# w_in of the first attention in two stages: 13 outputs summed over all k tiles as the modulation arrives, then the query blocks

## The chip, the cores and the metric

The kernel runs on one core of one Trainium2 chip. The metric is the device time of one execution in microseconds (us). All weights and activations are float32 in HBM; TensorE (PE) multiplies, VectorE (DVE) and ScalarE (ACT) work on SBUF and PSUM, SyncE (SP) issues the DMA transfers from one queue.

## The reference

Three layers run on 256 tokens of 2048 features. The first is the one that the change touches:

```python
mod = silu(c) @ w_mod + b_mod                     # c: one row of 2048; mod: 6 x 2048
sh1, sc1, g1, sh2, sc2, g2 = split(mod, 6)
h = rms_norm(x, norm_attn) * (1.0 + sc1) + sh1    # 256 x 2048
qa, ka, va, qb, ckv, qi, ki, wi = split(h @ w_in) # 2048 x 3664
out_a = swa_attention(qa, ka, va, sinks, rel_a)   # 16 heads of 64, window 128
out_b = dsa_attention(qb, rms_norm(ckv, kv_norm), w_uk, w_uv, qi, ki, wi, rel_b)
x = x + g1 * (concat(out_a, out_b) @ w_out)
h = rms_norm(x, norm_ffn) * (1.0 + sc2) + sh2
x = x + g2 * conv_ffn(h, w_up, conv_w, conv_b, w_down)
```

dsa_attention scores all keys with 16 index heads (qi, ki, wi), keeps the 64 best keys of each query, and attends to these with 16 heads. After this come a gMLP layer and an MLA layer with modulations of their own (from a second row c_2).

## The kernel before

Activations lie transposed: 16 tiles of 128 features by 256 tokens. To reach float32 accuracy at the speed of the rounded type, each operand is split in a high and a low part. Weights come in loads of 1 MB (`load`, five buffers with the tag raw, shared by all weights); `parts` splits 1024 columns with one ScalarE copy (L327) and one VectorE subtraction (L328); five buffers each hold high and low parts, two and a half blocks of weights. `product` then runs three matmuls per k tile of 128 and output block of 128 (L338 to L340). A full block of 128 outputs over 16 k tiles is 48 matmuls of 256 columns.

The modulation vectors are 14 vectors of 2048 (MODS), each 16 MB of weights. `mod_part` computes 128 entries of one: it loads 1 MB in the buffers with the tag raw and VectorE multiplies and sums it (L448). Eight of the 16 column groups of sc1, which the first product needs, are computed otherwise: `mod_first` multiplies the column c by w_first on PE, with one output row (L462, 32 matmuls of 512 columns, each in two passes as plain float32), and turns the row to columns with small matmuls (L472). `mod_rest` is the list of all other modulation parts, in the order of MODS; `step(rate)` takes so many parts of the list as the rate says at each weight block, `need(name)` takes all that is left of one vector. The parts issue their loads in the same SP queue as the weights.

`setup` computes sc1's and sh1's first eight column groups and the root of the mean square of x (squares on ScalarE, added on VectorE, L313; summed over partitions by PE, L303; then `rsqrt`, `diagonal`, `row`). `first_attention` runs w_in in two halves over k: 14 pairs of output blocks (`half_blocks`, w[0, i]) and the 80 outputs of ki and wi over k tiles 0 to 7, kept in SBUF (part); then, when the other halves of sc1 and sh1 are there, the same over k tiles 8 to 15 (`final`), and VectorE adds the first half (L738). In the second half the index scores (`index`), the selection (`top`), the attention generators (`attend`: scores and softmax, transposes, values with two heads in two halves of PE's columns, L644 and L646), and the keys and values of the second attention (`keys_of`, `values`) are worked in between the pairs. Two pairs of the second half run as plain float32 without a split (WIN). Then w_out runs in two halves with the second attention's eight head pairs in between, and the FFN opens with `shifts` and `opening`, whose first products have 258 columns and need all of sh2.

The program's framework orders the instructions of each engine at build time by a priority list and its own costs; each engine then works through its order, and a semaphore holds it where an operand or a buffer is missing.

Of the kernel before, what the change touches and what calls it, by code (L numbers as in the profile page):

```python
# [21 lines left out]
P = 128  # L22
# [16 lines left out]
WIN, WOB = (6, 8), (0, 2)  # L39
# [3 lines left out]
RP0, RP1, RWA, RWB, RF, RG, RM = 1.0, 1.7, 2.0, 1.0, 0.82, 0.5, 0.6  # L43
# [3 lines left out]

MODS = ["sc1", "sh1", "g1", "sc2", "sh2", "g2", "shA", "scA", "gA", "kvsh", "kvsc", "shB", "scB", "gB"]
# [11 lines left out]
def _layout(a):  # L60
# [19 lines left out]
    m["w_first"] = c(ws["sc1"][:, :1024].reshape(8, 2, P, 1024).transpose(0, 2, 1, 3)).reshape(8, P, 2048)  # L80
# [18 lines left out]
    for w in range(3):  # L99
# [18 lines left out]
    m["w_kiwi"] = c(kiwi.reshape(2, 8, P, 80).transpose(0, 2, 1, 3)).reshape(2, P, 8 * 80)  # L118
    m["w_in"] = c(np.concatenate([qi, ckv, ka, va, qa, qb], 1).reshape(2, 8, P, 14, 2, P).transpose(0, 3, 2, 4, 1, 5)
                  ).reshape(2, 14, P, 2048)  # L120
# [78 lines left out]
class Build:  # L199
# [253 lines left out]
    def mod_first(self):  # L453

        nc = self.nc
        banks = [self.bank(), self.bank()]
        for q in range(8):
            raw = self.load(self.ap["w_first"][q])
            for e in range(2):
                k = 2 * q + e  # L460
                for j in range(2):
                    nc.tensor.matmul(banks[j][:1], self.cact[:, k:k + 1],  # L462
                                     raw[:, e * 1024 + j * 512:e * 1024 + j * 512 + 512],
                                     start=k == 0, stop=k == 15)
            if q < 7:
                yield
        line = self.tmp("s", (1, 1024))
        for j in range(2):
            nc.scalar.copy(line[:, j * 512:j * 512 + 512], banks[j][:1])
        ps = self.bank()  # L470
        for b in range(8):
            nc.tensor.matmul(ps[:, b:b + 1], line[:, b * P:(b + 1) * P], self.ones[:1, :1], start=True, stop=True)  # L472
        nc.vector.tensor_add(self.mod_tile("sc1")[:, :8], ps[:, :8], self.vec("b_sc1", 0, 8))
        self.mod["sc1"][1] += 8
        yield

    def mod_rest(self):
        for j in range(8, DB):
            for name in ("sc1", "sh1"):
                self.mod_part(name, j)  # L480
                yield
        for name in MODS[2:]:
            for j in range(DB):
                self.mod_part(name, j)
                yield
# [167 lines left out]
    def setup(self):  # L653
# [4 lines left out]
        self.cact = self.con.tile([P, DB], F32, name="cact")  # L658
        nc.scalar.activation(self.cact, self.vec("c", 0, DB), AF.Silu)
        self.c_src = None  # L660
        a = self.mod_first()
        self.X = self.con.tile([P, DB, T], F32, name="X")
        self.acc = self.con.tile([P, T], F32, name="ssacc")
        for q in range(8):
            next(a)
            self.mod_part("sh1", q)
            if q == 1:
                nc.sync.dma_start(self.X, self.ap["xT"])
                self.ident = self.load_const("ident")
            if q == 3:  # L670
                for k in range(DB):
                    self.add_square(self.acc, self.X[:, k], k == 0)
                self.R = self.row(self.diagonal(self.rsqrt(self.token_sums(self.acc), 2, 1.0 / D)))
# [20 lines left out]
    def first_attention(self):  # L694
        nc, ap = self.nc, self.ap
        with self.tc.tile_pool(name="pa", bufs=1, reuse_waits="tile") as pool:
            g1a = self.gain(self.vec("norm_attn", 0, 8), self.mod_tile("sc1")[:, :8], "gg1a")
            xs = self.modulated(self.R, g1a, self.mod_tile("sh1"), range(8))
            w, wk = ap["w_in"], ap["w_kiwi"]
            isc = 64 ** -0.5 * 16 ** -0.5  # L700

            def kiwi(half, xs):
                raw = self.load(wk[half], 640)
                ps = self.bank()
                self.product(ps[:80], self.parts(raw, 0, 640), xs, width=80)
                self.step(0.6)
                return ps

            scale = lambda i: 0.125 if i >= 6 else 1.0
            ps = kiwi(0, xs)  # L710
            keys = self.pair()
            kw = keys[:80, 0]
            nc.scalar.activation(kw[:64], ps[:64, :T], AF.Copy)
            nc.scalar.activation(kw[64:], ps[64:80, :T], AF.Copy, scale=isc)
            part = []
            for i in range(14):
                pp = self.half_blocks(w[0, i], xs, RP0)
                part.append(self.pair())
                for e in range(2):
                    self.evac(part[i][:, e], pp[e], scale(i), which=1)  # L720
                if i == 3:
                    self.tables(pool)
            self.need("sc1"), self.need("sh1")
            g1b = self.con.tile([P, DB], F32, name="gg1b")
            nc.vector.scalar_tensor_tensor(g1b[:, 8:], self.mod_tile("sc1")[:, 8:], 1.0,
                                           self.vec("norm_attn", 8, 8), op0=OP.add, op1=OP.mult)
            xf = []
            xs = self.modulated(self.R, g1b, self.mod_tile("sh1"), range(8, 16), xf)
            rate = RP1
# [109 lines left out]
            for j in range(8):  # L839
# [17 lines left out]
                if j == 5:  # L857
                    keys_of(0)
# [474 lines left out]
```

## Time and profile before

| what | value |
|---|---|
| median of three runs | 2306.7 us (2305.6 to 2308.2) |
| profiled execution, its own time | 2308.6 us |
| its span, first to last instruction | 2306.9 us |
| busy PE, DVE, ACT | 97%, 81%, 50% of the span |
| mean granted clock of TensorE | 0.988 of full |
| DMA | 629.6 MB, 273 GB/s over the span |

The span leaves out 1.7 us of the execution's own time. Busy time counts pipelined matmuls from their start to a modelled end; a busy PE can still work at a lower granted clock, which is listed beside it. Lines with an L are lines of the kernel before. A matmul of plain float32 shows as two passes. In the rows of windows the busy times stand in the order PE, weight loads of PE (PEld), DVE, ACT, POOL, each with its count of instructions.

### The profile page before, as it was taken

Reading aid. Unit: us, or ns where it says so; the run is one execution under the profiler, and the core shown is the slowest. Engines: PE = TensorE matmul, PEld = TensorE weight load, DVE = VectorE, ACT = ScalarE, POOL = GpSimd, SP = SyncE. Lnnn points to the kernel's source line nnn. Section 1 sums busy time; section 2 is a strip of 40 time slices with the busy share of each in tenths; the row PEclk is TensorE's granted clock in tenths of the full one; section 3 lists DMA queues with packets and bytes.
Section 4 is the critical chain, followed back from the end, with each engine's and each line's share of the span. In section 5 each row is a group of like instructions: output and inputs, shape, how many; then the busy total and the mean of one; then the engine's idle time right before and its main releaser. Section 6 shows DMA issues by size and latency. Waiting matters only on the chain.

```text
span 2306.9 us, 42375 instructions
## 1 busy us (share of the span) xinstructions
PE 2248.1 (97%) x17326; PEld 2130.1 (92%) x17326; DVE 1869.0 (81%) x3043; ACT 1151.2 (50%) x1917; POOL 4.0 (0%) x8
## 2 busy tenths in 40 slices
PE   7988999999999999999999999999999999999999
PEld 1987888999999999999998889999999999899899
DVE  4889998999898888888898769777776568766784
ACT  2543675665444444444675444435344457455552
POOL 0000000000000000000000000000000000000000
PEclk8999999999999999999999999999999999999999
DMA  9898798889998999898677776887775555344342
GB/s 372 341 355 330 281 378 315 307 331 338 340 358 316 333 360 344 300 360 342 210 251 285 280 276 249 288 285 272 279 274 191 185 187 179 136 156 156 138 147 92
DMA packets 97764, 629.57 MB, mean 273 GB/s; under 512 B 10945, under 2 KB 18081, under 8 KB 28961
## 3 DMA queue, kind: packets, MB, share of 16 engines
q1 hardware_dynamic: 97570, 626.87, 73.7%
q8 instruction: 135, 2.21, 0.4%
q14 instruction: 59, 0.48, 0.1%
HBM read 624.68 MB, written 2.15 MB: 272 GB/s over the span
## 4 chain that ended last, share of the span: by engine, by line
PE 88%; DVE 8%; ACT 2%; issue 1%; DMA 1%; SPq 0%; DVEq 0%; ACTq 0%
PE bank L339 24%; PE bank L338 24%; PE bank L340 24%; PE bank L405 4%; PE bank L404 4%; PE bank L406 4%; DVE mraw L448 2%; DVE wl L328 2%; PE bank L462 1%; DMA raw<-in_w_first_dram 1%; PE bank L1019 1%; PE bank L594 1%; ACT wh L327 1%; PE bank L386 0%; DVE ssacc L313 0%
## 5 line engine op out<-in xcount | busy, mean ns | idle before, releaser
L338 PE MATMUL bank<-act,wh 128*128 128x256 f32 (+2 forms) x4976 | 1411.5, 284 | 15.3 <-ACT wh L327 9.3
L339 PE MATMUL bank<-act,wh 128*128 128x256 f32 (+1 forms) x4976 | 1405.4, 283 | 0.6 <-DVE act L259 0.3
L340 PE MATMUL bank<-act,wl 128*128 128x256 f32 (+2 forms) x4976 | 1399.0, 282 | 4.3 <-DVE wl L328 4.3
L327 ACT ACTIVATE wh<-raw 128x1024 fp32r<-128x1024 f32 (+2 forms) x760 | 759.9, 1007 | 672.7 <-PE bank L339 493.7
L328 DVE TENSOR_TENSOR wl<-raw,wh 128x1024 fp32r<-128x1024 f32 (+2 forms) x760 | 874.8, 1160 | 213.7 <-ACT wh L327 211.3
L338 PEld LDWEIGHTS bank<-act,wh 128*128 128x128 f32 (+1 forms) x4976 | 942.6, 190 | 24.7 <-ACT wh L327 10.8
L340 PEld LDWEIGHTS bank<-act,wl 128*128 128x128 f32 (+1 forms) x4976 | 941.4, 189 | 6.2 <-DVE wl L328 6.1
L339 PEld LDWEIGHTS bank<-act,wh 128*128 128x128 f32 (+1 forms) x4976 | 943.7, 190 | 1.9 <-DVE act L259 1.6
L448 DVE CUSTOM_DVE_ANT_0 mraw<-mraw,c_all,k_vecs 128x2048 f32<-128x2048 f32 x216 | 506.4, 2346 | 47.0 <-DMA mraw<-in_wmods_dram 25.9
L404 PE MATMUL bank<-wh,act 128*128 128x512 f32 (+1 forms) x392 | 152.0, 388 | 0.0
L405 PE MATMUL bank<-wl,act 128*128 128x512 f32 (+1 forms) x392 | 151.6, 387 | 0.0
L406 PE MATMUL bank<-wh,act 128*128 128x512 f32 (+1 forms) x392 | 151.1, 385 | 0.0
L258 ACT ACTIVATE act<-t 128x256 fp32r<-128x256 f32 x158 | 63.6, 414 | 95.5 <-DVE t L916 52.3
L404 PEld LDWEIGHTS bank<-wh,act 128*128 128x128 f32 x392 | 73.7, 188 | 15.5 <-PE bank L1223 1.0
L406 PEld LDWEIGHTS bank<-wh,act 128*128 128x128 f32 x392 | 73.7, 188 | 15.0 <-issue 0.7
L405 PEld LDWEIGHTS bank<-wl,act 128*128 128x128 f32 x392 | 73.8, 188 | 14.9 <-issue 0.7
L259 DVE TENSOR_TENSOR act<-t,act 128x256 fp32r<-128x256 f32 x158 | 64.7, 424 | 15.7 <-ACT act L258 15.1
L905 ACT ACTIVATE t<-bank,k_vecs 128x256 f32<-128x256 f32 x41 | 23.0, 560 | 70.6 <-PE bank L340 70.6
L567 DVE SCALAR_TENSOR_TENSOR X<-bank,m_g,X 128x256 f32<-128x256 f32 x96 | 46.1, 481 | 7.4 <-PE bank L340 5.3
L567 DVE SCALAR_TENSOR_TENSOR X<-bank,m_gA,X 128x256 f32<-128x256 f32 x64 | 30.8, 481 | 18.4 <-PE bank L340 18.4
L462 PE MATMUL bank<-raw,cact 128*1 128x512 f32 x64 | 36.1, 723 | 9.3 <-DMA raw<-in_w_first_dram 9.3
L909 ACT ACTIVATE t<-t 128x256 f32<-128x256 f32 x44 | 18.3, 416 | 52.4 <-DVE t L907 52.4
(230 smaller groups left out, 1214.4 us busy)
## 6 DMA issues: line engine op xcount, KB each, us to landing
mraw<-in_wmods_dram SPq DMA_DIRECT2D x216, 1024.0 KB, 6.6
raw<-in_w_up_dram SPq DMA_DIRECT2D x88, 1024.0 KB, 6.6
raw<-in_w_down_dram SPq DMA_DIRECT2D x64, 704.0 KB, 5.7
raw<-in_w_u_dram SPq DMA_DIRECT2D x32, 1024.0 KB, 5.2
raw<-in_w_v_dram SPq DMA_DIRECT2D x32, 1024.0 KB, 4.9
raw<-in_w_z_dram SPq DMA_DIRECT2D x32, 1024.0 KB, 5.0
raw<-in_w_ao_dram SPq DMA_DIRECT2D x32, 1024.0 KB, 4.9
raw<-in_w_in_dram SPq DMA_DIRECT2D x28, 1024.0 KB, 7.2
```

What stands on the lines that cost most here:

```text
L258: self.nc.scalar.activation(hi, src, AF.Copy)
L259: self.nc.vector.tensor_sub(lo, src, hi.bitcast(F32))
L327: nc.scalar.activation(h[:, :n], raw[:, lo:hi], AF.Copy)
L328: nc.vector.tensor_sub(l[:, :n], raw[:, lo:hi], h[:, :n].bitcast(F32))
L338: mm(ps[:, :n], h[:, s], x[:, :n], start=first and k == 0, stop=False)
L339: mm(ps[:, :T], h[:, s], x[:, LO:], start=False, stop=False)
L340: mm(ps[:, :n], l[:, s], x[:, :n], start=False, stop=last and k == len(xs) - 1)
L404: mm(ps, xh, h[:, s], start=k == 0, stop=False)
L405: mm(ps, xh, l[:, s], start=False, stop=False)
L406: mm(ps, xl, h[:, s], start=False, stop=k == kt - 1)
L448: self.nc.vector.tensor_tensor_reduce(out=raw, in0=raw, in1=self.c_all, scale=1.0, scalar=self.vec("b_" + name, j), op0=OP.mult, op1=OP.ad ...
L567: self.nc.vector.scalar_tensor_tensor(self.X[:, b], ps[:, :T], gate[:, b:b + 1], self.X[:, b], op0=OP.mult, op1=OP.add)
```

## The change

w_in is laid out anew. Its first 13 output blocks (index queries, compressed keys, k and v of the first attention, ki and wi) are w_a, one load of 1616 columns per k tile. Seven PSUM banks hold their sums over all 16 k tiles: `tile_of(k)` runs 39 matmuls for k tile k as soon as its operand is there, and sc1's and sh1's parts for k are loaded in between. Then 16 query blocks (w_q), each over all 16 k tiles, run one by one with index scores, selection and the first attention in between; keys and values of the second attention come after them. Half of sc1 and all of g1 are computed on PE by `mod_cols`: a load holds four k tiles by 512 columns, its four matmuls have 32 output rows each (one of them not zero) and write four 32-partition strips of one bank; small matmuls against a column of ones sum the strips and turn them to columns. The squares of x are summed by PE over k. The lists of steps follow: one part per query block, g1 first. In the cut diff, `modulated` scales k tiles and makes their operands, and `taken` copies a pair of sums out of PSUM.

```diff
-WIN, WOB = (6, 8), (0, 2)
+WOB = (0, 2)
-RP0, RP1, RWA, RWB, RF, RG, RM = 1.0, 1.7, 2.0, 1.0, 0.82, 0.5, 0.6
+RP, RWA, RWB, RF, RG, RM = 1.0, 2.0, 1.0, 0.82, 0.5, 0.6
+WA = 1024 + 256 + 128 + 128 + 80
+COLS = ["sc1", "g1"]
...
-    def mod_first(self):
+    def mod_cols(self, name, q):
...
+        bank = self.bank()
+        for i in range(4):
+            raw = self.load(self.ap["w_cols"][COLS.index(name), q, i])
+            for e in range(4):
+                nc.tensor.matmul(bank[32 * e:32 * e + 32], self.cact[:, 4 * i + e], raw[:, e * 512:e * 512 + 512],
+                                 start=i == 0, stop=i == 3)
+            if i < 3:
                 yield
-        line = self.tmp("s", (1, 1024))
-        for j in range(2):
-            nc.scalar.copy(line[:, j * 512:j * 512 + 512], banks[j][:1])
+        line = self.pair().rearrange("p a b -> p (a b)")
+        nc.scalar.copy(line, bank)
...
+        for b in range(4):
+            nc.tensor.matmul(ps[:, b:b + 1], line[:, b * P:(b + 1) * P], self.ones[:, :1], start=True, stop=True)
+        s = slice(4 * q, 4 * q + 4)
+        nc.vector.tensor_add(self.mod_tile(name)[:, s], ps[:, :4], self.vec("b_" + name, 4 * q, 4))
+        self.mod[name][1] += 4
...
     def mod_rest(self):
+            if name in COLS:
+                for q in range(4):
+                    yield from self.mod_cols(name, q)
...
-        a = self.mod_first()
...
-        for q in range(8):
+        a = self.mod_cols("sc1", 0)
+        for q in range(4):
             next(a)
             self.mod_part("sh1", q)
...
+            if q == 1:
+                ss = self.bank()
                 for k in range(DB):
-                    self.add_square(self.acc, self.X[:, k], k == 0)
-                self.R = self.row(self.diagonal(self.rsqrt(self.token_sums(self.acc), 2, 1.0 / D)))
+                    sq = self.tmp()
+                    nc.scalar.activation(sq, self.X[:, k], AF.Square)
+                    for tb in range(2):
+                        nc.tensor.matmul(ss[:, tb:tb + 1], sq[:, tb * P:(tb + 1) * P], self.ones[:, :1],
+                                         start=k == 0 and tb == 0, stop=k == DB - 1 and tb == 1)
+                self.R = self.row(self.diagonal(self.rsqrt(ss[:, :2], 2, 1.0 / D)))
...
-        self.cact = self.con.tile([P, DB], F32, name="cact")
+        self.cact = self.con.tile([P, DB, 32], F32, name="cact")
+        nc.vector.memset(self.cact, 0.0)
+        nc.scalar.activation(self.cact[:, :, 0], self.vec("c", 0, DB), AF.Silu)
...
+            sums = [self.bank() for _ in range(7)]
+
+            def tile_of(k):
+
+                raw = self.load(ap["w_a"][k], WA)
+                x = xs[k]
+                hl = [self.parts(raw, 0, 1024), self.parts(raw, 1024, WA)]
+                for i in (12, *range(12)):
+                    h, l = hl[i // 8]
+                    n = 80 if i == 12 else P
+                    s = slice(i % 8 * P, i % 8 * P + n)
+                    ps = sums[i // 2][:n, i % 2 * T:i % 2 * T + T]
+                    mm = nc.tensor.matmul
+                    mm(ps, h[:, s], x[:, :T], start=k == 0 and i % 2 == 0, stop=False)
+                    mm(ps, h[:, s], x[:, LO:], start=False, stop=False)
+                    mm(ps, l[:, s], x[:, :T], start=False, stop=k == DB - 1 and (i % 2 == 1 or i == 12))
+
+            modulated(range(4))
+            a = self.mod_cols("sc1", 1)
+            for k in range(4):
+                tile_of(k)
+                next(a)
+                self.mod_part("sh1", 4 + k)
+            modulated(range(4, 8))
+            self.tables(pool)
+            done = 4
+            for k in range(8, DB):
+                self.mod_part("sc1", k)
+                self.mod_part("sh1", k)
+                modulated(range(k, k + 1))
+                for _ in range(2):
+                    if done < k:
+                        tile_of(done)
+                        done += 1
+            tile_of(DB - 1)
+
...
-            part = []
-            for i in range(14):
...
-            def final(i, turned=False, between=None):
...
+            qis = [taken(i, True) for i in range(4)]
+            kv = taken(5, False)
+            ckv = taken(4, False)
...
+            def query(n, between=None):
+
+                if n % 2 == 0:
+                    q_pairs.append(self.pair())
+                ps = self.bank()
+                hl = self.weights(ap["w_q"][n], DB, rate)
+                self.product(ps, hl[0], xs[:8], True, False)
+                if between is not None:
+                    between()
+                self.product(ps, hl[1], xs[8:], False, True)
+                nc.scalar.activation(_turned(q_pairs[n // 2][:, n % 2]), _two(ps[:, :T]), AF.Copy, scale=0.125)
...
-            gens = [first(0), first(1)]
-            for j in range(8):
...
+            gens = []
+            for n in range(16):
+                p = n - 5
+                query(n, (lambda: next(gens[p])) if 0 <= p < 8 else None)
+                if 0 <= p < 8:
+                    mix.append(next(gens[p]))
+                if n < 4:
+                    index(n, qis[n])
+                elif n < 8:
+                    top(2 * n - 8)
+                    top(2 * n - 7)
...
+                if 3 <= n < 11:
+                    gens.append(first(n - 3))
+            keys_of(0)
+            gens.append(second(0))
+            values()
+            gens.append(second(1))
+            keys_of(1)
```

## Rows read from the trace of the kernel before

**Rows 1.** Windows: stretch, length, busy us of five engines, granted clock, DMA share, GB/s.

```profile
0.00:59.00 59.00, 43.83 (x94) 10.14 (x94) 29.54 (x53) 12.79 (x29) 0.20 (x4) 0.88 0.92 373
59.00:152.00 93.00, 87.29 (x698) 85.18 (x698) 78.41 (x87) 47.29 (x82) 0.00 (x0) 0.96 0.91 349
152.00:309.00 157.00, 137.43 (x1004) 121.35 (x1006) 152.04 (x331) 87.27 (x216) 0.00 (x0) 0.92 0.86 319
309.00:378.00 69.00, 67.91 (x562) 59.15 (x558) 64.09 (x138) 48.85 (x139) 0.00 (x0) 1.00 0.94 352
378.00:429.00 51.00, 48.54 (x357) 46.47 (x353) 47.73 (x73) 28.21 (x54) 0.00 (x0) 1.00 0.82 309
480.00:900.00 420.00, 420.00 (x3558) 420.00 (x3557) 374.97 (x448) 199.09 (x267) 0.00 (x0) 1.00 0.91 340
```

**Rows 2.** Timeline: start, length, engine, line, operation, count, [wait before and its releaser].

```profile
30.63 1.02 PE L303 MATMUL bank<-ones,ssacc 128*128 128x1 f32 x4 [3.71 <-DVE ssacc L313]
...
38.11 0.37 ACT L297 COPY row<-bank 128x256 f32<-128x256 f32 x1 [11.85 <-PE bank L295]
...
56.87 0.17 DVE L473 TENSOR_TENSOR m_sc<-bank,k_vecs 128x8 f32<-128x8 f32 x1 [0.42 <-PE bank L472]
...
59.39 0.34 PE L338 MATMUL bank<-act,wh 128*80 128x256 f32 x1 [2.56 <-ACT act L258]
...
155.80 0.50 PE L338 MATMUL bank<-act,wh 128*80 128x256 f32 x1 [7.47 <-ACT wh L327]
...
309.40 0.38 PE L338 MATMUL bank<-act,wh 128*128 128x256 f32 x1
...
428.91 0.39 PE L338 MATMUL bank<-act,wh 128*128 128x258 f32 x1 [1.85 <-ACT act L538]
```

**Rows 3.** The page's costliest groups, VectorE.

```profile
L328 DVE TENSOR_TENSOR wl<-raw,wh 128x1024 fp32r<-128x1024 f32 (+2 forms) x760 | 874.8, 1160 | 213.7 <-ACT wh L327 211.3
...
L448 DVE CUSTOM_DVE_ANT_0 mraw<-mraw,c_all,k_vecs 128x2048 f32<-128x2048 f32 x216 | 506.4, 2346 | 47.0 <-DMA mraw<-in_wmods_dram 25.9
...
L259 DVE TENSOR_TENSOR act<-t,act 128x256 fp32r<-128x256 f32 x158 | 64.7, 424 | 15.7 <-ACT act L258 15.1
```

**Rows 4.** Windows of 20 us: clock and DMA in busy stretches.

```profile
40.00:60.00 20.00, 14.58 (x46) 4.16 (x45) 10.57 (x15) 3.84 (x8) 0.00 (x0) 1.00 1.00 410
100.00:120.00 20.00, 18.82 (x159) 18.61 (x158) 15.37 (x14) 9.96 (x15) 0.00 (x0) 1.00 1.01 419
140.00:160.00 20.00, 11.30 (x84) 10.72 (x83) 17.86 (x25) 14.22 (x27) 0.00 (x0) 0.81 0.91 333
220.00:240.00 20.00, 14.45 (x90) 12.50 (x90) 19.97 (x73) 11.11 (x34) 0.00 (x0) 0.74 0.90 350
```

**Rows 5.** Timeline, PE: one load of w_first.

```profile
45.98 3.59 PE L462 MATMUL bank<-raw,cact 128*1 128x512 f32 x8 [0.95 <-DMA raw<-in_w_first_dram]
```

**Rows 6.** Timeline, PE: products in two column groups and the next form.

```profile
238.41 0.65 PE L644 MATMUL bank<-pT,va 128*64 128x256 f32 x4
238.89 0.39 PE L646 MATMUL bank<-pT,va 128*64 128x128 f32 x4
239.21 0.49 PE L585 MATMUL bank<-pair 64*128 64x128 f32 x4
```

**Rows 7.** Groups of instructions by line, VectorE, 152 to 309 us.

```profile
L448 DVE CUSTOM_DVE_ANT_0 mraw<-mraw,c_all,k_vecs 128x2048 f32<-128x2048 f32 x27 | 63.1, 2343 | 0.0
...
L738 DVE SCALAR_TENSOR_TENSOR pair<-bank,pair 128x256 f32<-128x256 f32 x28 | 11.6, 420 | 1.7 <-PE bank L340 1.4
```

**Rows 8.** Groups of instructions by line, VectorE, 309 to 428 us.

```profile
L448 DVE CUSTOM_DVE_ANT_0 mraw<-mraw,c_all,k_vecs 128x2048 f32<-128x2048 f32 x21 | 49.2, 2343 | 0.0
```

**Rows 9.** Timeline, SP: the first load of w_up.

```profile
412.53 0.33 SPq L319 DMA_DIRECT2D raw<-in_w_up_dram  x1
```

## What the change will do to the time

> **What bounds the kernel now.** I read the view by windows first, cut at the stage borders, because shares over the whole span hide that only the first fifth is not bound by TensorE. From 480 us on PE is busy all the time: 3558 matmuls in 420 us, 0.118 us each, so a full block of 48 costs 5.67 us [rows 1]. Nothing in the change touches that part, except one load more or less of lead. What the change can win lies ahead of 429 us, and the timeline gives the borders [rows 2]: the first product of w_in starts at 59.4, the second half of w_in at 155.8 (after 7.5 us of waiting), w_out at 309.4, the opening of the FFN at 428.9. Three things bind there. Up to 59 us it is transfers: 373 GB/s, and PE is busy with single-row sums. From 152 to 309 it is VectorE: 152.0 busy of 157, while PE stands still for 20 us and much of its busy time runs at a granted clock of 0.92 of full [rows 1]. From 309 to 429 PE binds again, 116.5 of 120 us, but VectorE is close behind it with 111.8 [rows 1]. So a gain ahead of 309 reaches the end, provided that VectorE does not get more to do behind 309.
>
> **The change part by part.** All times are on the span's clock; the profiled execution took 2308.6 us (span 2306.9), the median of the runs is 1.9 us lower.
>
> *Setup.* The modulation that the first product needs shrinks from eight loads of w_first and eight of sh1 to four and four. With X and the vectors that is 10.8 MB, 29 us at 373 GB/s [rows 1], where the old sums ended at 57.0 [rows 2]. The sum of squares leaves VectorE (15 additions) for 64 one-column passes on PE. Four such passes took 1.02 us at a low clock [rows 2], so they cost at most 16 us, beside loads. X lands earlier, as its load now stands ahead of the second block of w_cols; I let the squares begin at 16 and the sum end near 32. From there the old chain to the row of roots took 6.8 us (31.65 to 38.48) [rows 2]. With 2.5 us to the first operand (56.87 to 59.39 before) the first tile starts at 41 instead of 59.4. The roots, not the modulation, are then late.
>
> *First stage, w_in's 13 outputs.* PE needs 16 x 39 x 0.118 = 74 us, VectorE per late k tile two modulation sums of 2.35, splits of 1.2 and 0.7 and twice 0.42 for the operand [rows 3], 7.4 us. Loads: up to the fourth tile 22.5 MB in all, at 373 GB/s 60 us; then 16 blocks of modulation and 12 of w_a, 26.7 MB. Their rate lies between the 419 and the 333 GB/s of busy windows [rows 4]: 64 to 80 us; I take 370, 72 us, so that the last block lands at 132. Per k tile that is 7.9 us of transfer against 7.4 of VectorE and 4.6 of PE: the loads set the pace. Behind them stand one sum (2.35), the last operand (2.5), the last tile (4.6) and 1.5 us for a clock that falls in the gaps: the stage ends at 143 (135 to 152).
>
> *Second stage, queries.* The old window has 137.4 us of PE busy at a clock of 0.92, some 126 at full clock. Its 14 half products and the small one were 82, so index scores, attention, keys and values are 44 [rows 1]. The new stage has 16 blocks (90.7), the same 44, and gate g1: 16 loads of four matmuls, each to another 32 columns of the array. Nothing before writes four column groups, so I bound it. The upper end is the old form, one row: 3.59 us per load of eight passes [rows 5]. The lower end comes from attention's products, which write two column groups: four passes of 256 columns take 0.48 us until the next product starts, where the one-row form (0.449 per pass of 512) would take 0.90 [rows 5, 6]. So groups do run side by side; four groups make 0.96 per load. The shorter products behind them take 0.32 instead of half of 0.48 until a product of another form starts, 0.08 for the switch [rows 6]; two switches make 1.12 per load, 18 us. The Trainium skill speaks against the change here: TensorEngine Tiling (Array Packing), Key Properties, says that a change of tiling mode drains TensorE. The row agrees, at 0.08 us a time. With 3 us for the little products that turn g1 into columns, PE has 156 us. VectorE loses 27 modulation sums (63.1) and 28 additions (11.6) [rows 7] and gains eight splits (10): 87 of 157 us, no longer the bound. ScalarE's cost (copies out of PSUM instead of two evacuations) lies beside PE: it is busy 87 of 157 [rows 1]. I add 4 us of waits, as the old kernel has between 309 and 429 [rows 1], and take off 2 because query 0 needs only operands 0 to 7 for its first half and can fill the wait for the last one. w_out starts at 143 + 158 = 301 instead of 309.4.
>
> *The background list.* This is the price. Sixteen query steps use up exactly g1's sixteen loads. The sixteen of sc2 come in w_out's first half, eight of sh2 in its second, and the last eight are forced by need("sh2") right ahead of the FFN, in front of w_up on SP's queue. The old kernel ran 21 modulation sums behind 309 (49.2 us) [rows 8]; the new one must run 32, less what SP's five raw buffers let it do early. The weights of queries, keys and w_out that fill these buffers leave a sum little to wait for, so I take 8 done early. Then VectorE has 111.8 - 49.2 + 24 x 2.35 = 119.0 us beside PE's 119.5: two engines that are both full don't fit without loss; I take 5 us (0 to 18; 18 is with nothing early, 62.6 + 75.2 = 137.8). The queue says the same: w_up's first load left 16.4 us before its product started [rows 2, 9], and eight loads of 1.05 MB take 22.5 us at 373 GB/s.
>
> *Sum.* 301 + 119.5 + 5 = 425.5 against 428.9: 3.4 us earlier, the rest of 1878 us unchanged. 2308.6 - 3.4 = 2305.2 for an execution like the profiled one, 2303 for a median.
>
> **The rivals.**
> 1. *The forced loads bite* (slower). VectorE has done nothing early, so 13 us more stand ahead of the FFN: 2316. For it: VectorE is 94% busy from 378 on [rows 1] and SP issues in order. Against it: PE sets the pace of the second stage, so sums that need only VectorE should run ahead there. It decides against the change below about six sums done early: (32 - 6) x 2.35 + 62.6 is 4 us over PE's time, and with the 5 us of friction that eats the 8.4 won before.
> 2. *The column groups don't overlap*, so that gate g1 costs PE what mod_first did: 16 x (3.59 - 1.12) = 40 us more, 2343. The two-group rows speak against it [rows 6].
> 3. *Loads run at the upper rate* and VectorE has slack. At 410 to 419 GB/s [rows 4] the blocks land 13 us earlier, VectorE then holds the stage to 7 of these, and the FFN opens without the 5 us: 2290. For it: such rates stand where only large rows move. Against it: five buffers, shared by weights that wait for PE.
> 4. *The clock falls in the first stage.* Where PE was busy 14.5 of 20 us the granted clock was 0.74, and 0.81 around the wait of 7.5 us [rows 4]; at 0.74 a tile takes 6.2 us, still under the 7.9 between tiles, and only the last one counts. At the low level, 1.2 GHz, a tile takes 9.2 us, and five late tiles and the last one lose 5 x 1.3 + 4.6 = 11 us: 2313. The Trainium skill, TensorE: Matmul & The Clock Gate, HAM oscillation, tells of a loop over k tiles with a transfer to wait for that runs every tile cold; the old kernel's rows fall only in part.
>
> **How the numbers follow.** 0.2% of this kernel, 4.6 us, is about what a measurement tells from no change. The forecast, 2303, has 0.50; its own terms (end of the first stage 135 to 152, opening 0 to 9) spread it over 0.24 faster, 0.22 same, 0.04 slower. Rival 1 has 0.18, rival 2 0.07, rival 3 0.17, rival 4 0.08 (0.02 of it same). That makes faster 0.41, same 0.24, slower 0.35. The range leaves out rival 2 and the tail beyond rivals 1 and 3: 2286 to 2324; the forecast's own range is 2292 to 2313, since its two terms seldom stand at the same end.
>
> **What would show it.** In the new profile: the first product of a tile near 41; the last tile's end near 143 with a DMA share over 0.9 until then; four one-row matmuls of a load within about 1.1 us (rival 2: 3.6); VectorE under 65% busy in the queries, PE over 95%; residuals of w_out starting near 304; the wait ahead of the 258-column products under 7 us (rival 1: 15 or more). I am wrong if the planner's order holds TensorE on a load or a bank that this arithmetic does not see, above all in the first stage, where seven of eight banks are taken.

## The result: 40 us slower

The changed kernel takes 2346.3 us (median of 4 runs, 2345.8 to 2347.9) against 2306.7 (2305.6 to 2308.2): a ratio of 1.0173, interval 1.0155 to 1.0190. The forecast was 2303, range 2286 to 2324. It failed, and the sign with it: a gain was forecast, and the kernel is 1.7% slower.

The windows of the changed kernel, cut at its own stage borders (setup, first stage, queries, w_out, and the stretch behind 480 that [rows 1] also has):

```profile
0.00:49.00 49.00, 30.89 (x115) 19.02 (x116) 15.33 (x35) 14.57 (x33) 0.20 (x4) 0.97 0.75 292
49.00:166.00 117.00, 93.08 (x674) 84.86 (x677) 88.55 (x111) 42.00 (x69) 0.00 (x0) 0.87 0.91 349
166.00:330.00 164.00, 158.82 (x1272) 132.66 (x1265) 99.14 (x267) 98.17 (x242) 0.00 (x0) 0.98 0.73 264
330.00:466.00 136.00, 114.89 (x904) 104.65 (x902) 128.04 (x216) 73.84 (x182) 0.00 (x0) 0.94 0.90 333
480.00:900.00 420.00, 419.41 (x3547) 418.93 (x3546) 376.30 (x468) 208.29 (x289) 1.67 (x2) 1.00 0.90 335
```

Behind 480 nothing has changed. The queries are TensorE's, as forecast (158.8 busy of 164). The first stage is nobody's: PE 93, VectorE 89 of 117 us, 349 GB/s. From w_out on VectorE leads, 128.0 of 136.

The borders in the changed kernel's timeline answer [rows 2]. The second line is the first residual of w_out, which began 3.2 us after w_out's first product before (312.6 and 309.4), so that w_out starts near 329.6 (an estimate from these rows):

```profile
48.78 0.50 PE L728 MATMUL bank<-act,wh 128*80 128x256 f32 x1 [4.72 <-ACT wh L331]
332.76 0.45 DVE L568 SCALAR_TENSOR_TENSOR X<-bank,m_g,X 128x256 f32<-128x256 f32 x1
466.02 0.58 PE L342 MATMUL bank<-act,wh 128*128 128x258 f32 x1 [20.99 <-ACT act L539]
```

First tile 48.8 (forecast 41), w_out 329.6 (301; 309.4 before), opening of the FFN 466.0 (425.5; 428.9 before). The opening is 37.1 us late, the spans differ by 37.2: all of the loss lies ahead of 466. (The medians differ by 39.7: the profiled execution of before stood 1.9 above its median, that of the change 0.6 below.) Of the 37.1, 20.2 stand at w_out's start and 16.9 come between there and the opening.

**Three places where it goes.** First, setup. VectorE's timeline:

```profile
18.53 0.22 DVE L683 CAST identb<-k_ident 128x128 bf16<-128x128 f32 x1
32.38 0.16 DVE L271 TENSOR_SCALAR rs_x<-bank 128x2 f32<-128x2 f32 x1 [13.63 <-PE bank L678]
...
34.23 2.35 DVE L452 CUSTOM_DVE_ANT_0 mraw<-mraw,c_all,k_vecs 128x2048 f32<-128x2048 f32 x1
...
47.31 0.08 DVE L452 DVE_READ_ACCUMULATOR2_ANT m_sh<- 128x1 f32 x1
```

The first operation of the root waits 13.6 us for the squares' sums on TensorE, at its place in VectorE's fixed order, and sh1's second sum stands behind it. Its raw buffer stays held, and the loads stop: SP issues only three from 8.6 to 36.6. The row of roots came when forecast (38.8), but sh1's fourth sum was done only at 47.3.

Second, the late k tiles: VectorE, ScalarE and SP's queue in one period of 8.60 us (from one k tile's multiply-add on ScalarE, L519, to the next one's):

```profile
115.15 0.33 SPq L323 DMA_DIRECT2D raw<-in_w_a_dram  x1
...
123.83 2.35 DVE L452 CUSTOM_DVE_ANT_0 mraw<-mraw,c_all,k_vecs 128x2048 f32<-128x2048 f32 x1
...
126.22 0.60 ACT L519 ACTIVATE t<-t,m_sh,gg 128x256 f32<-128x256 f32 x1 [6.15 <-DVE m_sh L452]
126.73 1.04 ACT L331 ACTIVATE wh<-raw 128x1024 fp32r<-128x1024 f32 x1
...
127.80 1.23 DVE L332 TENSOR_TENSOR wl<-raw,wh 128x1024 fp32r<-128x1024 f32 x1 [1.27 <-ACT wh L331]
```

The w_a tile issued at 115.15 lands some 6.2 us later, at 121.4 (the next one, issued at 123.75, can't be the one split at 126.7). ScalarE is idle, but at the head of its order stands the multiply-add of the next operand, which waits for VectorE's sum until 126.2. Then VectorE waits 1.27 us for wh; that is nearly all the idle time it has in the period, and with its own 7.3 us of work it makes the 8.60. The tile holds one of five raw buffers meanwhile.

Third, the opening. SP's queue, whose w_up load left at 412.5 before [rows 9]:

```profile
421.48 0.33 SPq L323 DMA_DIRECT2D raw<-in_w_out_dram  x1
425.31 28.19 SPq L449 DMA_DIRECT2D mraw<-in_wmods_dram  x9
455.44 11.87 SPq L323 DMA_DIRECT2D raw<-in_w_up_dram  x6
```

Nine modulation loads in a row, paced by VectorE's sums through the raw buffers, and w_up behind them: TensorE stands 21.0 us. What ends the wait is the last sum of sh2 and not w_up: ScalarE has split the first w_up load from 460.8 on, and then waits for VectorE to make the operand of the 258-column products from sh2:

```profile
464.54 0.22 ACT L536 ACTIVATE shift<-m_sh 128x16 fp32r<-128x16 f32 x1 [2.69 <-DVE m_sh L452]
```

### The profile page after: what moved, and what is told of

Its sections match the earlier page's. It is cut to its first block, busy times and chain, and to the rows that moved or that the text cites. A ratio compares the mean times of both kernels' runs of the same rounds, so it can differ in the third digit from the quotient of the medians.

```text
span 2344.1 us, 42822 instructions
## 1 busy us (share of the span) xinstructions
PE 2261.0 (96%) x17578; PEld 2148.6 (92%) x17578; DVE 1826.3 (78%) x2989; ACT 1155.0 (49%) x1926; POOL 4.9 (0%) x8
## 4 chain that ended last, share of the span: by engine, by line
PE 81%; DVE 5%; ACT 1%; issue 1%; ACTq 0%; DVEq 0%
PE bank L342 22%; PE bank L343 22%; PE bank L344 22%; PE bank L408 4%; PE bank L409 4%; PE bank L410 4%; DVE mraw L452 1%; DVE wl L332 1%; PE bank L1048 1%; DVE X L568 0%; PE bank L1245 0%; PE bank L595 0%; ACT wh L331 0%; PE bank L390 0%; PE bank L603 0%
## 5 line engine op out<-in xcount | busy, mean ns | idle before, releaser
L342 PE MATMUL bank<-act,wh 128*128 128x256 f32 (+1 forms) x4800 | 1360.9, 284 | 22.5 <-ACT act L539 21.0
L343 PE MATMUL bank<-act,wh 128*128 128x256 f32 x4800 | 1352.7, 282 | 0.7 <-DVE act L263 0.6
L344 PE MATMUL bank<-act,wl 128*128 128x256 f32 (+1 forms) x4800 | 1350.6, 281 | 0.0
L331 ACT ACTIVATE wh<-raw 128x1024 fp32r<-128x1024 f32 (+3 forms) x770 | 764.4, 1001 | 704.2 <-PE bank L343 493.4
L332 DVE TENSOR_TENSOR wl<-raw,wh 128x1024 fp32r<-128x1024 f32 (+3 forms) x770 | 879.0, 1152 | 247.8 <-ACT wh L331 245.8
L342 PEld LDWEIGHTS bank<-act,wh 128*128 128x128 f32 x4800 | 908.3, 189 | 36.7 <-ACT act L539 21.2
L343 PEld LDWEIGHTS bank<-act,wh 128*128 128x128 f32 x4800 | 909.2, 189 | 1.7 <-DVE act L263 1.3
L344 PEld LDWEIGHTS bank<-act,wl 128*128 128x128 f32 x4800 | 907.5, 189 | 0.1
L452 DVE CUSTOM_DVE_ANT_0 mraw<-mraw,c_all,k_vecs 128x2048 f32<-128x2048 f32 x200 | 469.1, 2348 | 44.2 <-DMA mraw<-in_wmods_dram 28.3
L728 PE MATMUL bank<-act,wh 128*128 128x256 f32 (+1 forms) x208 | 61.0, 304 | 26.9 <-ACT wh L331 26.8
L263 DVE TENSOR_TENSOR act<-t,act 128x256 fp32r<-128x256 f32 x166 | 68.2, 424 | 17.1 <-ACT act L262 16.3
L728 PEld LDWEIGHTS bank<-act,wh 128*128 128x128 f32 (+1 forms) x208 | 41.9, 203 | 32.1 <-ACT wh L331 30.5
L729 PE MATMUL bank<-act,wh 128*128 128x256 f32 (+1 forms) x208 | 59.9, 298 | 0.0
L730 PE MATMUL bank<-act,wl 128*128 128x256 f32 (+1 forms) x208 | 56.7, 304 | 0.3 <-DVE wl L332 0.3
```

Of the source, the lines that this page charges most:

```text
L263: self.nc.vector.tensor_sub(lo, src, hi.bitcast(F32))
L331: nc.scalar.activation(h[:, :n], raw[:, lo:hi], AF.Copy)
L332: nc.vector.tensor_sub(l[:, :n], raw[:, lo:hi], h[:, :n].bitcast(F32))
L342: mm(ps[:, :n], h[:, s], x[:, :n], start=first and k == 0, stop=False)
L343: mm(ps[:, :T], h[:, s], x[:, LO:], start=False, stop=False)
L344: mm(ps[:, :n], l[:, s], x[:, :n], start=False, stop=last and k == len(xs) - 1)
```

## The experiments

**1. Spread the owed vectors.**

```diff
-RP, RWA, RWB, RF, RG, RM = 1.0, 2.0, 1.0, 0.82, 0.5, 0.6
+RP, RWA, RWB, RF, RG, RM = 1.5, 2.0, 1.0, 0.82, 0.5, 0.6
```

> Only RP goes from 1.0 to 1.5: the 16 queries draw 24 steps of the modulation instead of 16, so that 8 sums of sc2 move from the w_out stretch into the queries, where the load queue had slack (258 to 279 GB/s). Theory (the vectors that are still owed when w_out starts hold back w_up's loads): the wait ahead of the 258-column products falls from 21.0 us to under 8 us, total 2328 to 2334 against 2346. Rival (VectorE and the loads are full in both stretches, the wait only moves): the queries grow by as much as the opening gains, total 2343 to 2349.

2333.1 us, ratio 1.0115 (1.010 to 1.013), 13 less than the change. TensorE's first 258-column product with its wait (21.0 in the change, 1.85 in [rows 2]):

```profile
450.36 0.39 PE L342 MATMUL bank<-act,wh 128*128 128x258 f32 x1 [1.84 <-ACT act L539]
```

19 of the 21 us of waiting are gone, so the sums forced in front of the opening, with their loads, were the cause. The first residual moved from 332.8 to 336.1: 3 us were paid in the queries.

**2. The store off SP's queue.**

```diff
-        nc.sync.dma_start(self.bias, bt)
+        nc.gpsimd.dma_start(self.bias, bt)
```

> Only the store of the bias table is issued from POOL instead of SP. Theory (SP's in-order queue stands from 68.6 to 78.4 us behind this store, which waits for a TensorE product that waits for the eighth bank): loads go on in that gap, TensorE's 10.2 us wait at 88 shrinks below 4 us, the first stage ends 6 to 9 us earlier, total 2337 to 2341. Rival (the five raw buffers are full by then and the tiles are paced by VectorE's sums): the gap in the issues closes but the last tile ends within 2 us of 164, total 2344 to 2348.

2345.6, ratio 1.0170 (1.0153 to 1.0187); the last block of the last tile begins at 163.4 against 164.1. The rival was right. The store that held SP for 9 us cost next to nothing: with it gone, a load behind it waits 7.1 us for VectorE instead, as SP's waits show:

```profile
SPq L449 <- DVE act L263: 7.1, 1, 7.1
```

TensorE's longest wait in the first stage, which the theory put on the store, falls only from 10.2 to 9.1 us (first the change, then this kernel):

```profile
87.96 0.58 PE L728 MATMUL bank<-act,wh 128*128 128x256 f32 x1 [10.17 <-ACT wh L331]
```

```profile
87.32 0.58 PE L728 MATMUL bank<-act,wh 128*128 128x256 f32 x1 [9.13 <-ACT wh L331]
```

Both end with ScalarE's wh, which stands behind a multiply-add that waits for VectorE's sum, 5.9 us in the change and 4.6 here: the same order as in the late k tiles.

**3. The root later in the program.**

```diff
-            if q == 1:
+            if q == 3:
                 ss = self.bank()
```

> Only the place of the root in the program changes: the squares, their sums by TensorE and the root stand behind the fourth sum of sh1 instead of the second, so that VectorE's order has sums 3 and 4 ahead of the root's first operation. Theory (VectorE waits 13.6 us in order on the squares' sums, its raw buffers stay held, and only 3 loads are issued from 8.5 to 36.6 us): loads go on, the first tile begins 5 to 8 us before 48.8, the first stage ends about that much earlier, total 2338 to 2342. Rival (later pacing by VectorE's sums absorbs an early start): first tile earlier, last tile within 2 us of 164, total 2344 to 2348.

2351.2, ratio 1.0192 (1.0177 to 1.0207): 5 us more than the change, though the two intervals overlap; in any case no gain, and neither theory. The first tile begins at 52.3, the last block at 166.8. In this kernel's timeline of TensorE and VectorE:

```profile
30.75 13.79 PE L678 MATMUL bank<-ones,t 128*128 128x1 f32 x64
...
44.58 0.16 DVE L271 TENSOR_SCALAR rs_x<-bank 128x2 f32<-128x2 f32 x1 [13.00 <-PE bank L678]
```

The sums of sh1 did come first (18.9, 24.0 and 28.9), but all 64 passes of the squares went behind the last columns of sc1, and the wait of 13 us only moved. The passes themselves are the trouble, some 14 us of TensorE in either place (9.6 + 4.4 in the change, 13.8 here).

**4. g1 by VectorE again.**

```diff
-COLS = ["sc1", "g1"]
+COLS = ["sc1"]
```

> Only g1 goes back to VectorE's sums (16 x 2.35 us there), sc1's columns stay with TensorE. Theory of the prediction (16 loads of g1 cost TensorE 1.06 to 1.1 us each, and TensorE sets the pace of the queries at 97%): w_out starts 16 to 19 us earlier than 329.6, total 2326 to 2332 if the opening's wait does not grow; with less time for the same sums ahead of the opening it may take back up to 8, 2338. Rival (VectorE, 36 to 38 of 40 us busy in parts of this stretch, becomes the pace): w_out starts less than 8 us earlier, total 2338 to 2350.

2328.8, ratio 1.0099 (1.0084 to 1.0114), 17.5 less. The group of w_out's residuals, with its first and last start:

```profile
L568 DVE SCALAR_TENSOR_TENSOR X<-bank,m_g,X x9: 456/480/486, 313.3 to 348.0; 128x256 f32<-128x256 f32 x9
```

w_out starts 19.5 us earlier, where the forecast had priced g1 on TensorE at 18 + 3. The wait at the opening stays (19.9).

**5 and 6. Fewer loads, or shorter sums.** In the fifth kernel

```diff
-                self.mod_part("sc1", k)
-                self.mod_part("sh1", k)
+                self.mod_part("sh1", k, self.mod_part("sc1", k))
```

(the sum of sh1's call is taken over the buffer that the other one loaded, so sc1's second half is not computed), in the sixth

```diff
-                self.mod_part("sc1", k)
+                self.mod_part("sc1", k, 256)
```

> Leaves out the loads of sc1's last 8 vectors: their sums are taken over the buffer that sh1's load filled (so sc1's second half is not computed); the sums themselves stay. 1 MB of 2.8 MB less for each k tile. Theory (VectorE and ScalarE's chain paces the late tiles: two sums, multiply, and the wait for wh, 8.6 us per k tile): the period of k=11 to 15 stays 8.4 to 8.6 us. Rival, the forecast's (the loads set the pace): it falls to about 5.5 to 7.4.

> Leaves out work, not loads: sc1's last 8 vectors are loaded whole, but each is summed over 256 of its 2048 elements only (about 0.35 us instead of 2.35). Theory (the chain of VectorE and ScalarE paces): the period of k=11 to 15 falls from 8.6 to 7.4 to 7.9 us, where 2.83 MB at 370 GB/s (7.6 us) hold it, and the last tile is done 9 to 12 us earlier (two-tile periods of 10.4 us included). Rival (the loads pace already): it stays at 8.4 to 8.6.

Windows over late periods, three of the changed kernel and four each of the fifth and the sixth (columns as in [rows 1]):

```profile
117.00:143.00 26.00, 19.03 (x129) 18.13 (x127) 22.07 (x28) 7.33 (x12) 0.00 (x0) 0.87 0.96 344
```

```profile
112.00:141.00 29.00, 23.49 (x194) 22.79 (x192) 29.00 (x40) 13.04 (x20) 0.00 (x0) 1.00 0.76 275
```

```profile
114.00:142.00 28.00, 23.60 (x185) 21.86 (x184) 22.24 (x38) 9.77 (x16) 0.00 (x0) 1.00 1.01 417
```

The period is 7.1 us without the loads (VectorE 29.00 of 29.00) and 6.9 with shorter sums (417 GB/s). (One run each, 2332.2 and 2335.1 us; both kernels leave out work, so their totals price no mend.)

The fifth expectation failed: 7.1 lies in its rival's range. But the kernel is not a clean cut. With the loads gone, the tiles were split so far ahead that VectorE waits for no wh in the window, so loads and wait went together; here the wh was done at 115.0 (VectorE's timeline):

```profile
119.46 1.91 DVE L332 TENSOR_TENSOR wl<-raw,wh 128x1024 fp32r<-128x1024 f32 x2
```

The sixth tells them apart. All loads are still issued and run at 417 GB/s where the change draws 344, so they do not set the pace of 8.6. One sum is 1.87 us shorter (0.48 for 2.35) and 1.7 of it come off the period, while the wait for wh stays:

```profile
122.92 1.23 DVE L332 TENSOR_TENSOR wl<-raw,wh 128x1024 fp32r<-128x1024 f32 x1 [1.28 <-ACT wh L331]
```

So the chain of VectorE's work (7.1 to 7.3 us) and its wait for ScalarE paces the late tiles. Experiments 8 and 9 try to take the wait away with all work and loads kept.

**7. The squares on VectorE, as before.**

```diff
-                    sq = self.tmp()
-                    nc.scalar.activation(sq, self.X[:, k], AF.Square)
-                    for tb in range(2):
-                        nc.tensor.matmul(ss[:, tb:tb + 1], sq[:, tb * P:(tb + 1) * P], self.ones[:, :1],
-                                         start=k == 0 and tb == 0, stop=k == DB - 1 and tb == 1)
+                    self.add_square(self.acc, self.X[:, k], k == 0)
```

> The squares go back to the accumulation of before (ScalarE squares, VectorE adds, one column sum at the end); everything else is the changed kernel. Theory (TensorE's 64 passes at the low clock, 16.6 to 32.3 us, hold VectorE's order 13.6 us and with it the raw buffers and the loads): VectorE needs 15 x 0.4 us from X's landing at 16, the root is ready near 27, row near 30 to 32 instead of 38.8, loads go on, the first tile begins at 42 to 44 instead of 48.8 and the last tile ends 4 to 7 us earlier; total 2339 to 2342. Rival (later pacing absorbs it): last tile within 2 us of 164, total 2344 to 2348.

2339.7, ratio 1.0134 (1.0117 to 1.0151), 6.7 less. VectorE's additions in this kernel, and the group of the first product of every block of the tiles (the last start is that of the last tile's last block):

```profile
20.06 7.30 DVE L317 TENSOR_TENSOR ssacc<-ssacc,t 128x256 f32<-128x256 f32 x14
```

```profile
L723 PE MATMUL bank<-act,wh x208: 274/282/582, 41.8 to 159.9; 128*128 128x256 f32 x95, 128*80 128x256 f32 x9
```

The first tile begins at 41.8, 7 us earlier, and the last block of the last tile 4.2 us earlier (159.9 against 164.1).

**8. Split the tile earlier in the program.** The load and the split of the due tiles (one or two) are written ahead of the two sums.

```diff
+                todo = [(d, tile_parts(d)) for d in range(done, min(done + 2, k))]
                 self.mod_part("sc1", k)
                 self.mod_part("sh1", k)
+                for d, hl in todo:
+                    tile_of(d, hl)
                 modulated(range(k, k + 1))
```

> In the late tiles the load and the splitting of a w_a tile stand ahead of the two modulation sums in the program, its products behind them; nothing else is changed. Theory (ScalarE's wh stands in order behind the modulated block that waits for VectorE's second sum, and VectorE then waits 1.27 us for wh in each k tile): the wait goes, the period of k=11 to 15 falls from 8.6 to 7.4 to 7.8 us, the last tile is done 6 to 10 us earlier, total 2336 to 2341. Rival (the raw buffers are five: a tile loaded earlier holds one and the sums' loads come later): period 8.4 or more, total 2345 to 2352.

2345.2, ratio 1.0160 (1.0145 to 1.0175): a gain that can't be told from none. The planner laid ScalarE's late instructions in the same order as before, the multiply-add still waits 6.16 us ahead of wh, and the period is still 8.60 (ScalarE's timeline):

```profile
127.78 0.60 ACT L519 ACTIVATE t<-t,m_sh,gg 128x256 f32<-128x256 f32 x1 [6.16 <-DVE m_sh L452]
128.28 1.04 ACT L331 ACTIVATE wh<-raw 128x1024 fp32r<-128x1024 f32 x1
```

The edit did not reach the order it was meant to change, so it says nothing on the theory.

**9. Split the tile one k tile ahead, and hold the multiply-add behind it.**

```diff
+            done, todo = 4, [tile_parts(4)]
...
+                while n and done < k:
+                    tile_of(done, todo.pop(0))
+                    done, n = done + 1, n - 1
+                    if done + len(todo) < DB:
+                        todo.append(tile_parts(done + len(todo)))
+                with self.tc.issue_after(self.last_wh):
+                    modulated(range(k, k + 1))
```

> In the late tiles each w_a tile is loaded and split one k tile earlier, and ScalarE's multiply-add of the modulated block (which waits for VectorE's second sum) is queued behind that tile's wh instead of ahead of it; nothing else changes. Theory (a landed tile waits on ScalarE behind that multiply-add, VectorE then waits 1.27 us per k tile for wh, and the tile holds a raw buffer meanwhile): VectorE's wait goes, the period of k=11 to 15 falls from 8.6 to 7.0 to 7.5 us, the last tile is done 6 to 11 us before 164, total 2335 to 2341. Rival (five raw buffers: with one more held ahead, the sums' loads come late instead, or the loads themselves need 7.9 us): period 7.9 or more, last tile less than 4 us earlier, total 2342 to 2350.

2334.1, ratio 1.0113 (1.0099 to 1.0127), 12 less. A window over four late periods, the group of the blocks' first products, and ScalarE's timeline:

```profile
119.00:147.00 28.00, 20.15 (x156) 18.52 (x156) 28.00 (x36) 11.21 (x17) 0.00 (x0) 1.00 1.02 420
```

```profile
L731 PE MATMUL bank<-act,wh x208: 274/281/579, 49.1 to 151.4; 128*128 128x256 f32 x92, 128*80 128x256 f32 x12
```

```profile
122.34 1.65 ACT L331 ACTIVATE wh<-raw 128x1024 fp32r<-128x1024 f32 x2 [4.35 <-DMA raw<-in_w_a_dram]
123.91 0.60 ACT L519 ACTIVATE t<-t,m_sh,gg 128x256 f32<-128x256 f32 x1
```

With the same sums and the same bytes VectorE has no idle time left, the loads run at 420 GB/s, and the period is 7.1 us (the multiply-adds begin at 123.91, 131.01 and 138.12). The cause of the lost time per k tile was the order on ScalarE. TensorE's wait of 10.2 us at 88 is 3.5 here (until 82.8).

Not all of the 12.7 us by which the last block comes earlier is that wait. The eight periods from the multiply-add at 79.4 (81.2 here) to the last one give 8.5 us, less 1.8 for their later start. The other 5.9 come behind the last multiply-add, from 12.1 us to 6.2: the tiles are split ahead, and none is left to split there. The last multiply-adds, of the change and of this kernel:

```profile
152.00 0.60 ACT L519 ACTIVATE t<-t,m_sh,gg 128x256 f32<-128x256 f32 x1 [6.15 <-DVE m_sh L452]
```

```profile
145.23 0.60 ACT L519 ACTIVATE t<-t,m_sh,gg 128x256 f32<-128x256 f32 x1 [0.23 <-DVE m_sh L452]
```

**10 to 12. The mends together.** The tenth kernel is the change with RP 1.5, the seventh's squares and the ninth's order. The eleventh has g1 by VectorE on top. The twelfth splits g1, 8 vectors to each engine:

```diff
             if name in COLS:
-                for q in range(4):
+                for q in range(2):
                     yield from self.mod_cols(name, q)
-            else:
-                for j in range(DB):
-                    self.mod_part(name, j)
-                    yield
+            for j in range(8 if name in COLS else 0, DB):
+                self.mod_part(name, j)
+                yield
```

> The change kept whole, with three mends together: RP 1.5, squares as in the kernel before, and w_a tiles split ahead of the modulated block. Theory (three separate losses, the setup's held loads, the late tiles' chain, the vectors owed at the opening): their gains add, 13 + 7 + 6 to 10, total 2316 to 2321 against 2346. Rival (a gain in one place comes back as a wait in the next): the sum of the gains is under 18, total over 2328.

> As c1_all, and g1 summed by VectorE again, so that of the change the two stages of w_in and half of sc1 by TensorE stay. Theory (g1's 16 loads cost TensorE 17 to 19 us in queries that TensorE paces, and VectorE still has the time for them): 15 to 18 below c1_all, total 2299 to 2306, at or under the 2306.7 of before. Rival (16 sums more of 2.35 us, with the 8 that RP 1.5 brings forward, fill VectorE in the queries): 5 or less below c1_all, total 2311 or more.

> As the kernel with all three mends and g1 by VectorE, but g1's first 8 vectors come as columns by TensorE (8 loads, 8 to 9 us of TensorE), the other 8 by VectorE (19 us of VectorE less). Theory (in that kernel VectorE is the later of the two from 150 us to the opening: TensorE waits there 9 us for it in the queries and 10 us from w_out to the opening): the waits fall by 12 to 16 us and 9 are paid, total 2299 to 2304, below the 2306.7 of before. Rival (TensorE's price is paid in full and the waits stay, since they hang on the order of VectorE's sums and not on their number): total 2307 to 2315.

| kernel | us | ratio to before, interval | last tile's last block begins | first residual |
|---|---|---|---|---|
| change | 2346.3 | 1.0173 (1.0155 to 1.0190) | 164.1 | 332.8 |
| mends | 2310.9 | 1.0010 (1.0000 to 1.0019) | 148.9 | 318.8 |
| mends, g1 by VectorE | 2306.6 | 0.9993 (0.9984 to 1.0002) | 146.7 | 299.1 |
| mends, half of g1 | 2304.5 | 0.9986 (0.9977 to 0.9995) | 144.8 | 298.5 |

The gains add: against 466.0 in the change the opening begins 15.6 us earlier in experiment 1 (450.4), 4.5 in 7 (461.5) and 14.2 in 9 (451.8), and with all three 33.0 (433.0). The total, 2310.9, lies 5 us under the expected range.

Moving g1 is worth 17.5 us alone and 4 with the mends, as the rival said: with 16 sums more, VectorE is busy 138.0 of the 145 us from 150 to 295, where it had 96.9 in the tenth kernel. w_out starts 20 us earlier, and the opening only 7 (the tenth kernel, then the eleventh):

```profile
433.02 0.39 PE L342 MATMUL bank<-act,wh 128*128 128x258 f32 x1 [1.83 <-ACT act L539]
```

```profile
426.10 0.39 PE L342 MATMUL bank<-act,wh 128*128 128x258 f32 x1 [3.01 <-ACT act L539]
```

TensorE's waits from 150 to 435 us in the eleventh kernel, by what ended them (total, times, longest):

```profile
PE bank L344 <- DVE wl L332: 8.2, 8, 1.8
PE bank L595 <- ACT s L638: 7.5, 3, 3.8
PE bank L342 <- ACT act L539: 3.0, 1, 3.0
```

The same view of the twelfth:

```profile
PE bank L344 <- DVE wl L332: 4.7, 5, 1.2
PE bank L342 <- ACT act L538: 3.0, 1, 3.0
PE bank L472 <- ACT pair L469: 2.0, 2, 1.3
```

These waits fall from 18.7 to 9.7 us, by 9 and not by the 12 to 16 expected, and TensorE pays half of g1 for it; the total missed its range by 0.5 us. The half split lies 0.14% under the kernel before, less than the bound named in the prediction; its interval leaves out 1 by little, and it overlaps that of the eleventh kernel, so which of the two splits is better is not shown.

## Why the prediction was wrong

- **"The roots, not the modulation, are then late", first tile at 41.** The sum of squares (32) and the row (38.8) came as worked out. The modulation was late because VectorE's order put the root, waiting 13.6 us, ahead of three sums of sh1. I had sized the 64 passes rightly (at most 16 us; they took 14) and then costed them at nothing, "beside loads"; the loads were what they stopped. Without them the tile begins at 41.8 (experiment 7). Loss: 7.8 us here.
- **"The loads set the pace", 7.9 us per k tile.** This step failed twice. Loads could do 420 GB/s, 2.92 MB in 7.0 us (rival 3 had that and VectorE as the next bound right). And neither they nor VectorE's 7.4 (measured 7.1) set the pace of 8.6 (10.4 where two tiles fall in one period): VectorE's work with a wait for ScalarE of 1.27 us in each k tile did, which the sum had left out; experiment 9 shows that ScalarE's order was its cause. The sign named for loads that set the pace, a DMA share over 0.9, was there all the same (0.91 in the stage, 0.96 in the late tiles at 344 GB/s), so it can't tell them from loads that wait. With that order right, the stage from 49.1 to 151.4 lasts the 102 us that I had worked out from wrong terms. That the stage so mended meets the forecast's length is luck. The last sentence of the prediction named the planner's order as the danger, but on TensorE, with a load or a bank as the reason; TensorE's wait of 10.2 us at 88 hung on ScalarE's order too (9.1 without the store, 3.5 in experiment 9). Loss: 13.5 us.
- **Second stage, 158 us.** It took 165, from 164.3 to 329.6: 2.3 us until the first query's product at 166.6, 3.2 of waits for ScalarE's copies ahead of g1's little products and 1.7 of one wait for ScalarE in attention (L595), where the forecast had 2 us for all waits; PE is 97% busy. Rival 2 is refuted, though its 2343 is near the time: the eight passes of a load take 1.07 us, as in this row of the changed kernel's timeline, beside 3.59 in [rows 5]:

```profile
174.00 1.07 PE L464 MATMUL bank<-raw,cact 128*32 128x512 f32 x8
```

  g1's price was sized rightly, 18 + 3 against 19.5 (experiment 4). Of it the passes make 17.1. Behind the load at 174.00 the first product starts at 175.00 and the next 0.22 us later, where 0.12 is their pace. But products behind L595's, which have all 128 columns, lose as much (332.72 to 332.92), so neither this nor the 0.08 us that the prediction read from [rows 6] is the price of a change of mode alone. What a switch to the four-group form costs by itself was not measured, so the drain of which the Trainium skill tells (TensorEngine Tiling (Array Packing), Key Properties) is bounded by these numbers and not shown.
- **The background list, "8 done early", 5 us.** Mis-sized, and the sign of the whole hung on it. The windows of the sums alone (each counts two instructions; then clock, DMA share, GB/s):

```profile
165.00:200.00 35.00, 0.00 (x0) 1.00 0.76 279
200.00:329.60 129.60, 9.41 (x8) 0.97 0.71 258
329.60:466.00 136.40, 65.59 (x56) 0.94 0.90 334
```

  Ahead of w_out 4 sums were done and 28 came behind, so VectorE had 62.6 + 65.6 = 128.2 us (128.0 busy) beside PE's 119.5, and the stretch took 136.4 (forecast 124.5). So 8 early were 4 too many, and the sum took VectorE as never idle, where it stood still for 8 us. Rival 1 was the right mechanism, at 0.18; its wait is 21.0 ("15 or more"), and 19 of it go with one number (experiment 1). Its price, 13 us over the forecast's opening, was right too (12); that the first stage would be late as well stood in no rival. So few sums were early because sixteen query steps are spent on g1's sixteen loads, and sc2's stand behind these in the list: idle time of VectorE could not draw them forward.
- **What held.** VectorE is not the bound in the queries (99 of 164 us, 60%; forecast 87 of 157). A gain ahead of 309 reaches the end only if VectorE has no more to do behind it: the mends show just that, since an earlier w_out is paid back at the opening. Of rival 4 there is a part: the granted clock was 0.87 in the first stage. It went with the waits (1.00 in the late tiles of experiment 9), and what it cost beside them is not shown.

In sum the forecast lost 21 us in the first stage, 7 in the second and 12 up to the opening: the 40.5 between 425.5 and 466.0.

What stays open: what the eighth bank costs by itself, how much of the fifth kernel's gain is its order, and what part of the first stage's loss is the lower clock.

## What to carry to other kernels

A pace worked out from bytes and busy time holds only if no engine's fixed order puts an instruction that waits ahead of one that is ready; so for each late operand ask what stands in front of its first consumer on that engine, and which buffer it holds meanwhile. Moving work off a full engine moves the list that was hidden behind it too: count what is still owed at each border, by the order in which the queue is filled, not by the idle time of the engine that will do it. And a program edit meant to reorder an engine has to be seen in that engine's order before its time means anything (experiments 8 and 9).

## What the hardware showed beyond that

- One in-order queue drew 420 GB/s over 28 us with 1 MB and 0.8 MB loads (experiment 9), where the same loads gave 344 when a k tile's buffers came free every 8.6 us instead of 7.1; a rate read from a window with waits is no limit.
- The eight passes of a column load took 1.93 us in setup (row below) and 1.07 at 174 us, though the granted clock of 0 to 49 us stands at 0.97, and at 1.00 from 16 to 31 us, where experiment 7's expectation speaks of the low clock. This view does not show why the early products run at nearly half the pace.

```profile
6.53 1.93 PE L464 MATMUL bank<-raw,cact 128*32 128x512 f32 x8 [6.53 <-DMA raw<-in_w_cols_dram]
```
